# Seven block products for eight in every projection of a pooling and mLSTM layer, with the mLSTM core as a stage of its own

## The chip, the core and the metric

The kernel runs on one core of a Trainium2 chip. The metric is device time in microseconds (us); lower is better. Every time here is that of one launch, and the profile shows one execution. The five engines are TensorE (PE; its weight loads are PEld), VectorE (DVE), ScalarE (ACT), GpSimd (POOL) and SyncE (SP), which issues all DMAs of both kernels.

## The reference, cut

One layer on x, 4096 rows by 1024 channels. A norm, one input projection of five column blocks, two branches, one output projection, a residual and a final norm.

```
proj = rmsnorm(x, norm_w) @ w_in                  # 1024 -> 5 * 1024
pool_x, pool_z, m_x, m_z, m_o = split(proj)       # 1024 columns each
y_pool  = pool_mixer(pool_x, ...) * silu(pool_z)  # trailing means of 2/4/8/16 rows, a map per group
xc = silu(causal_conv(m_x, 4 taps));  q, k, v = small block maps of xc, xc, m_x
h  = mlstm_chunkwise(q, k, v, gates)              # 4 heads of 256, chunks of 128 rows, state handed on
y_mlstm = (headnorm(sigmoid(m_o) * h) + m_skip * xc) * silu(m_z)
out = rmsnorm(x + concat(y_pool, y_mlstm) @ w_out, final_norm_w)
```

So there are seven products of a 4096 by 1024 matrix with a 1024 by 1024 one: five into the branches, two (the halves of w_out) out of them.

## The kernel before, in words

Each float32 operand of a large product is split into a high part (a rounded copy, made by ScalarE) and a low part (the rest, a subtraction on VectorE): `split`, L88 to L90. `mm3` (L114 to L120) then issues three matmuls per pair of 128 by 128 stationary and 128 by 512 moving tiles: high by high, high by low, low by high. L118, L119 and L120 are these three. One of the seven products takes 8 row blocks of 512, 8 column tiles of 128, 8 k tiles and 3 parts, 1536 matmuls 512 wide.

Three stages follow one another, with DRAM between them.

* **Pooling mixer** (L140 to L304). Per block b of 512 rows and column tile j: 24 matmuls for pool_x, into which the group's map is folded beforehand (`fold`, L215), and 24 for pool_z. ScalarE evicts; VectorE makes the window sums (L280), subtracts (L288), multiplies by the gate (L292); POOL carries 16 columns of halo from block to block (L269, L270). `norm_u` (L157) normalises the next block in the background and stores it as `u_d`.
* **mLSTM** (L306 to L689). Per half block of 256 rows `project` makes m_x with matmuls 256 wide (192 of them), and `tail` and `silu` make x_c: three taps by SCALAR_TENSOR_TENSOR on VectorE (L370), SiLU by three functions on ScalarE (L394 to L396) and a product (L397). Per chunk of 128 rows `front` (L462) makes maps (L472, L482), scores (L493), gates, scans (L524, L526) and the decay factors (L552, L561), and `back` (L580) the numerator (L599, L603), the state (L628, L629) and its split copy (L355, L356). `ORDER` (L32) interleaves the steps of a chunk's front (f), the back of the chunk before (b), the next projection (p) and its convolution (c). The tile `qg` exists once: L484 fills it, L493 and L570 read it.
* **Gates, head norm, output** (L691 to L819). m_z and m_o in blocks of 512 rows, sigmoid as tanh, the head norm (L749 to L760), transposes (L726), then the output projection: per 128 rows and 512 columns 48 matmuls, VectorE adds the residual straight from PSUM (L804).

The order of the text sets the priority, not the order on an engine: the framework schedules the instructions when the program is built, and puts an instruction ahead of earlier ones that it expects to be still waiting. Each engine, SP with its DMA issues too, then takes its own list strictly in that order.

## Time and profile before

| | |
|---|---|
| three runs | 3156.46, 3160.59, 3160.87 us; median 3160.59 |
| profiled execution | span 3157.9 us; the page gives no time of its own for it beside the span, which lies 2.7 us under the median |
| pooling mixer | 0 to about 755 us |
| mLSTM | about 755 to 1732 us, 32 chunks |
| gates, head norm | about 1732 to 2443 us |
| output projection | about 2443 to 3158 us |
| mean granted TensorE clock | 0.986 |

How to read it: "busy" is the time in which an engine had an instruction running. Matmuls overlap one another, so the sum of their durations is more than the time they take, and the pace is read from how many start in a stretch. `x` before a number is a count. A row of the windows view gives, for one stretch of time, the length, then for PE, PEld, DVE, ACT and POOL the busy time and the count, then the granted clock, the share of time in which the DMA engines were busy, and GB/s.

### The profile page before, as it was taken

The numbers are of one execution on the slowest core, as the hardware profiler recorded it, in microseconds if no ns is written. First come the engines' busy times: TensorE is split into PE (matmuls) and PEld (weight loads), VectorE is DVE, ScalarE is ACT, GpSimd is POOL, SyncE is SP. The second block draws the span as 40 slices with busy tenths as digits, with TensorE's granted clock in tenths as the row PEclk, the third lists the DMA queues.
The fourth block names the chain that finished last, engine by engine and source line by source line (L and its number), as shares of the span: only waits on it lengthen the run. The fifth ranks groups of instructions, "written<-read, shape, count | busy, mean of one in ns | idle before, by whom it ended". The sixth has DMA issues, their size and how long they took to land.

```text
span 3157.9 us, 44492 instructions
## 1 busy us (share of the span) xinstructions
PE 3056.9 (97%) x16872; PEld 2659.8 (84%) x16872; DVE 1642.0 (52%) x3726; ACT 1162.2 (37%) x2464; POOL 573.8 (18%) x811
## 2 busy tenths in 40 slices
PE   7999999999899999999999999999999999999999
PEld 6888888888898998998998888888888788888887
DVE  5554444544788788888887443334436422222221
ACT  4221122223677677767776222222113311111111
POOL 1010010101354445444543000000000000000000
PEclk9999999999999999999999999999999999999999
DMA  6221111222111111112133223333215523222231
GB/s 210 87 77 70 61 67 60 77 97 75 61 55 58 51 54 62 50 51 64 51 91 112 76 93 107 107 107 107 68 59 173 184 100 107 94 92 96 94 107 50
DMA packets 189607, 273.57 MB, mean 87 GB/s; under 512 B 17232, under 2 KB 111952, under 8 KB 189392
## 3 DMA queue, kind: packets, MB, share of 16 engines
q1 hardware_dynamic: 189392, 270.72, 25.5%
q8 instruction: 133, 2.18, 0.3%
q14 instruction: 82, 0.67, 0.1%
HBM read 168.96 MB, written 101.71 MB: 86 GB/s over the span
## 4 chain that ended last, share of the span: by engine, by line
PE 86%; DVE 6%; DMA 3%; ACT 3%; issue 1%; SPq 1%; POOL 0%; POOLq 0%; DVEq 0%; ACTq 0%
PE acc L118 24%; PE acc L119 24%; PE acc L120 24%; DVE xc L370 3%; PE mm L603 2%; PE mm L628 2%; PE map L482 2%; PE mm L599 1%; DMA sk<-xc_d 1%; PE map L472 1%; PE map L493 1%; DMA ws<-in_w_out_dram 1%; PE acc L236 1%; DVE c L629 1%; PE tp L726 0%
## 5 line engine op out<-in xcount | busy, mean ns | idle before, releaser
L118 PE MATMUL acc<-u,w 128*128 128x512 f32 (+1 forms) x2592 | 907.3, 351 | 3.8 <-ACT mx L617 1.7
L120 PE MATMUL acc<-u,w 128*128 128x512 f32 (+1 forms) x2592 | 897.5, 346 | 0.0
L119 PE MATMUL acc<-u,w 128*128 128x512 f32 (+1 forms) x2592 | 895.5, 346 | 0.0
L118 PE MATMUL acc<-w,u 128*128 128x512 f32 x1536 | 598.4, 390 | 3.8 <-ACT w L89 2.8
L119 PE MATMUL acc<-w,u 128*128 128x512 f32 x1536 | 598.1, 390 | 0.2 <-DVE w L90 0.2
L120 PE MATMUL acc<-w,u 128*128 128x512 f32 x1536 | 597.5, 390 | 0.0
L118 PEld LDWEIGHTS acc<-u,w 128*128 128x128 f32 x2592 | 495.2, 191 | 64.2 <-ACT u L89 4.1
L119 PEld LDWEIGHTS acc<-u,w 128*128 128x128 f32 x2592 | 495.7, 191 | 58.6 <-DVE u L90 1.1
L120 PEld LDWEIGHTS acc<-u,w 128*128 128x128 f32 x2592 | 495.5, 191 | 57.4
L118 PEld LDWEIGHTS acc<-w,u 128*128 128x128 f32 x1536 | 288.5, 188 | 65.5 <-ACT w L89 3.6
L120 PEld LDWEIGHTS acc<-w,u 128*128 128x128 f32 x1536 | 288.9, 188 | 60.4 <-DVE u L790 0.6
L119 PEld LDWEIGHTS acc<-w,u 128*128 128x128 f32 x1536 | 288.6, 188 | 60.6 <-DVE w L90 0.7
L370 DVE SCALAR_TENSOR_TENSOR xc<-mx,col,xc 128x256 f32<-128x256 f32 x384 | 220.6, 632 | 30.5 <-POOL mx L447 22.3
L804 DVE TENSOR_TENSOR st<-acc,st 128x512 f32<-128x512 f32 x64 | 44.3, 692 | 364.9 <-PE acc L120 364.9
L356 POOL TENSOR_TENSOR cs<-c,cs 128x516 fp32r<-128x516 f32 x124 | 176.4, 1423 | 232.0 <-ACT cs L355 208.2
L757 POOL TENSOR_TENSOR rs<-rs,nhalf 128x2 f32<-128x2 f32 x64 | 44.6, 697 | 660.6 <-DVE rs L756 660.6
L789 ACT CAST u<-u 128x512 fp32r<-128x512 f32 x128 | 77.6, 619 | 230.7 <-PE acc L119 187.2
L811 ACT ACTIVATE sk<-st 128x1024 bf16<-128x1024 f32 x31 | 32.8, 1058 | 311.4 <-DVE st L804 311.4
L815 POOL TENSOR_TENSOR rso<-ssq,nhalf 128x1 f32<-128x1 f32 x32 | 17.4, 543 | 701.9 <-DVE ssq L812 701.9
L749 DVE SCALAR_TENSOR_TENSOR st<-th,st 128x512 f32<-128x512 f32 x64 | 44.3, 692 | 184.8 <-ACT th L747 184.7
L747 ACT ACTIVATE th<-acc 128x512 f32<-128x512 f32 x64 | 38.3, 598 | 273.4 <-PE acc L120 272.9
L599 PE MATMUL mm<-va,st 128*128 128x258 f32 x384 | 82.1, 310 | 52.3 <-DVE st L90 39.8
(181 smaller groups left out, 4201.9 us busy)
## 6 DMA issues: line engine op xcount, KB each, us to landing
u<-u_d SPq DMA_DIRECT2D x128, 256.0 KB, 3.9
st<-in_x_t_dram SPq DMA_DIRECT2D x32, 512.0 KB, 3.5
u_d<-st SPq DMA_DIRECT2D x32, 512.0 KB, 4.2
yp_d<-sg SPq DMA_DIRECT2D x64, 256.0 KB, 2.0
xc_d<-xc SPq DMA_DIRECT2D x64, 256.0 KB, 2.4
st<-h_d SPq DMA_DIRECT2D x32, 512.0 KB, 5.2
sk<-xc_d SPq DMA_DIRECT2D x64, 256.0 KB, 3.8
ym_d<-sg SPq DMA_DIRECT2D x64, 256.0 KB, 3.1
```

The source lines that it names most:

```text
L118: nc.tensor.matmul(ps, lhsT=a[0], rhs=b[0], start=start and k == 0, stop=False)
L119: nc.tensor.matmul(ps, lhsT=a[0], rhs=b[1], start=False, stop=False)
L120: nc.tensor.matmul(ps, lhsT=a[1], rhs=b[0], start=False, stop=stop and k == n - 1)
L356: nc.gpsimd.tensor_tensor(out=t[:, 1], in0=cst[h], in1=t[:, 0].bitcast(F32), op=ALU.subtract)
L370: nc.vector.scalar_tensor_tensor(out=a[:, t], in0=m[:, t, i:i + TB], scalar=conv_w[:, jj * 4 + i:jj * 4 + i + 1], in1=a[:, t], op0=ALU.mul ...
L482: nc.tensor.matmul(ps[:, i, :], lhsT=bqk[:, q * 4 + i, :], rhs=xc[q * 4 + i][:, l0:l0 + P], start=True, stop=True)
L599: nc.tensor.matmul(nps, lhsT=wt[:, w, h, :], rhs=vh[v], start=i == 0, stop=first and i == 2)
L603: nc.tensor.matmul(nps, lhsT=qi[h][:, w, t, :], rhs=cs[:, v, t], start=False, stop=t == 1 and i == 2)
L628: nc.tensor.matmul(upd, lhsT=xw[h][:, w, t * P:(t + 1) * P], rhs=vh[v], start=i == 0, stop=i == 2)
L749: nc.vector.scalar_tensor_tensor(out=hv, in0=th, scalar=1.0, in1=hv, op0=ALU.add, op1=ALU.mult)
L757: nc.gpsimd.tensor_tensor(out=rs, in0=rs, in1=nhalf[:, 0:2], op=ALU.pow)
L789: nc.scalar.copy(out=hi, in_=raw)
```

## The change

All seven products become block products of one Strassen-Winograd level: the left matrix is cut into row and k halves (1024 rows are one round r, so there are four rounds), the right one into k and column halves; seven products of sums of blocks replace eight products of blocks. A `Pass` is one product of 1024 columns (or of a mixture of columns) with seven resident, split weight blocks; `drive` streams the seven sums of the left operand past them. In one pass there are 4 rounds of 14 steps (7 block products, 2 k halves each), a step has 4 tiles q, 2 k tiles and 3 parts: 24 matmuls 512 wide.

Seven passes in this order: gate (pool_z); mix 0 and mix 1, each with half the columns of pool_x and half of m_x, whose items do the pooling, the convolution and SiLU; out 1 (upper half of w_out, added to x, stored as `r_d`); then the mLSTM core alone, which reads m_x and x_c from DRAM (`mx_d`, `xc_d`) and writes `h_d`; then head (m_o, sigmoid, head norm), z (m_z, transposes, skip, product) and out 2 (lower half of w_out, added to `r_d`, final norm). The sums of weights (`stage`) and of left operands (`put_left`) are formed on POOL (in the first norms on VectorE), stored in DRAM and loaded again. `ORDER` loses its p and c steps, and its f and b are arranged anew; `front` and `back` are otherwise as before, with three small changes: their inputs are slices of a loaded block, `mm` has 4 PSUM buffers for 3, `ht` has 2 for 1.

The core of the diff:

```
+A_OF = ("a11", "s2", "a12", "s3", "s1", "a22", "s4")
+B_OF = ("b11", "t2", "b21", "t3", "t1", "t4", "b22")
+AHEAD = 3
...
+            for k in range(0, 4, 2):
+                raw = lo[:, k:k + 2].bitcast(F32)
+                nc.sync.dma_start(out=raw, in_=self.wt_d[i][:, k:k + 2, :])
+                split(raw, hi[:, k:k + 2], lo[:, k:k + 2])
...
+    def drive(passes, ring, w2p, psp, background, after=None):
...
+        def fetch(t):
+            n, r, i, kh = steps[t]
+            hi = ring.tile([P, 2, T], F32R, name="sr")
+            lo = ring.tile([P, 2, T], F32R, name="sr")
+            raw = lo.bitcast(F32)
+            nc.sync.dma_start(out=raw, in_=passes[n].left[r][i][:, 2 * kh:2 * kh + 2, :])
+            split(raw, hi, lo)
...
+            for v in range(t, min(t + AHEAD, len(steps))):
+                if v not in got:
+                    fetch(v)
...
+            chain = "abab" "cbc"[i]
...
+            for q in range(4):
...
+                mm3(ps, pairs, start=kh == 0 and i in (0, 1, 4), stop=kh == 1, skip=True)
+                if kh == 1:
+                    f = p.items[q].after(r, i, ps)
...
+            if i == 0:
+                self.s1 = self.tile()
+                nc.scalar.copy(out=v(self.s1), in_=ps)
+            elif i == 1:
+                self.u2 = self.tile()
+                nc.vector.tensor_tensor(out=v(self.u2), in0=ps, in1=v(self.s1), op=ALU.add)
+            elif i == 2:
+                return self.done(r, 0, 0, self.first(ps))
...
+                elif (rh, ch) == (0, 1):
+                    self.mix(r, 0, 1, t)
+                    self.mix(r, 1, 1, self.u3)
+                    v = self.view
+                    put_left(yp_d[r], self.c, v(self.c11), v(t), v(self.s1), v(self.u3), xp, nc.gpsimd)
...
+                for i in range(3):
+                    nc.vector.scalar_tensor_tensor(out=a, in0=m[:, HALO - 3 + i:HALO - 3 + i + T],
...
+        norm_first()
+        for _ in p_gate.stage(xp, nc.gpsimd):
+            pass
+        for g in range(H):
+            fold(g)
+        for i in range(NP):
+            p_gate.load(i, w2p)
...
+            if n == 0 and r + 1 < NR:
+                for _ in range({0: 1, 1: 1, 2: 1, 3: 1, 6: 1, 7: 1, 8: 1, 9: 1, 10: 2}.get(m, 0)):
+                    next(norms[r])
+            if n < 3 and m in ((11, 12) if n == 0 else (4, 11)):
+                next(staged)
+
+        drive([p_gate, *p_mix, p_out1], ring, w2p, psp, background, p_o)
...
+        drive([p_o, p_z, p_out2], ring, w2p, psp, lambda n, r, m: None)
```

`stage` takes, per k tile of a half, 4 loads, 4 sums and 7 stores of 128 by 512 tiles, and has four such k steps per pass; `put_left` takes 4 sums and 7 stores. A fetch is one DMA and one split of 128 by 1024 elements; the ring holds four of them, and three are asked for ahead. The seven products of a round accumulate in three groups of four PSUM banks, "a", "b" and "c": products 0 and 2 in a, 1, 3 and 5 in b, 4 and 6 in c. An item evicts after each product: product 0 and 2 by ScalarE, the others by an addition on VectorE. A quadrant of the result is done after products 2, 4, 5 and 6. A pooling item mixes its first quadrant after product 2, the second after product 5 and the last two after product 6; with a window of 2 a quadrant takes 2 VectorE operations (in the first round more), with 4, 8 and 16 it takes 4, 5 and 6. A convolution item handles its quadrants in the same places: halo on POOL, one ScalarE operation, three SCALAR_TENSOR_TENSOR 512 wide, SiLU, and four DMAs. In the last round of a pass the next pass's seven weight blocks are loaded and split.

`norm_next(r)` loads the 16 tiles of a round's x twice, once for the sums of squares (squares on ScalarE, sums on POOL) and once to scale them (VectorE) and form the seven sums (VectorE). A gate item stores silu(pool_z) in `sz_d`, where the pooling items read it.

More of the change, by code (lines that the diff above doesn't have):

```diff
@@ L116, in mm3, with split @@
+    wf_d = [dram.tile([P, D], F32, name=f"wf_d{k}") for k in range(NJ)]
+    def split(raw, hi, lo, eng=None):
+        nc.scalar.copy(out=hi, in_=raw)
+        (eng or nc.vector).tensor_tensor(out=lo, in0=raw, in1=hi.bitcast(F32), op=ALU.subtract)
+    def mm3(ps, pairs, start=True, stop=True, skip=False):
         n = len(pairs)
         for k, (a, b) in enumerate(pairs):
-            nc.tensor.matmul(ps, lhsT=a[0], rhs=b[0], start=start and k == 0, stop=False)
-            nc.tensor.matmul(ps, lhsT=a[0], rhs=b[1], start=False, stop=False)
@@ new lines, in put_left, with new, put @@
+    def put_left(dst, k, a11, a12, a21, a22, pool, eng, shape=None):
+        def new():
+            return pool.tile([P, T], F32, name="x")
+        def put(what, t):
+            nc.sync.dma_start(out=dst[A_OF.index(what)][:, k, :], in_=t)
+        put("a11", a11)
+        put("a12", a12)
+        put("a22", a22)
+        s1 = new()
+        eng.tensor_tensor(out=s1, in0=a21, in1=a22, op=ALU.add)
+        s2 = new()
+        eng.tensor_tensor(out=s2, in0=s1, in1=a11, op=ALU.subtract)
+        put("s2", s2)
+        eng.tensor_tensor(out=a21, in0=a11, in1=a21, op=ALU.subtract)
+        put("s3", a21)
+        put("s1", s1)
+        s4 = new()
+        eng.tensor_tensor(out=s4, in0=a12, in1=s2, op=ALU.subtract)
+        put("s4", s4)
@@ new lines, in tile_hybrid, with stages, background @@
+        p_out2 = Pass("o2", ym_d, halves(out_rows(D), 0), [], True)
+        def stages():
+            for p in (*p_mix, p_out1, p_o, p_z, p_out2):
+                yield from p.stage(xp, nc.gpsimd)
+        norm_first()
+        for _ in p_gate.stage(xp, nc.gpsimd):
+            pass
+        for g in range(H):
+            fold(g)
+        for i in range(NP):
+            p_gate.load(i, w2p)
+        norms = [norm_next(r) for r in range(1, NR)]
+        staged = stages()
+        def background(n, r, m):
+            if n == 0 and r + 1 < NR:
[3 more added lines that the diff above has]
+                next(staged)
@@ new lines, in block @@
+        def block(b):
+            m = inp.tile([P, NJ, TB], F32, name="mx")
+            nc.sync.dma_start(out=m, in_=mx_d[b])
+            c = inp.tile([P, NJ, TB], F32, name="xc")
+            nc.sync.dma_start(out=c, in_=xc_d[b])
+            return m, c
+        bk = None
+        blocks = {0: block(0)}
+        with tc.issue_after(table.ins):
+            for n in range(NC + 1):
+                if n % 2 == 0 and n + 2 < NC:
+                    blocks[n // 2 + 1] = block(n // 2 + 1)
+                fr = Steps(front(n, n % 2, *blocks[n // 2]), 13) if n < NC else None
+                turn = {"f": fr, "b": bk}
+                for what in ORDER[n % 2]:
+                    if turn[what] is not None:
+                        turn[what].step()
+                if bk is not None:
+                    bk.finish()
+                if fr is None:
+                    break
+                bk = Steps(back(n, *fr.finish()), 5 if n + 1 == NC else 13)
+                bk.step()
@@ L822 @@
+        p_o.items = [Head(q) for q in range(4)]
+        p_z.items = [Mixed(c) for c in range(4)]
+        p_out2.items = [Final(q, r_d, out) for q in range(4)]
+        for i in range(4, NP):
+            p_o.load(i, w2p)
+        drive([p_o, p_z, p_out2], ring, w2p, psp, lambda n, r, m: None)
 def kernel(**inputs):
```

853 lines of the change are left out of this document (432 added, 421 removed).

## The prediction

> **What bounds the kernel now.** I read the page first, its engine line, slices and chain.
>
> ```profile
> span 3157.9 us, 44492 instructions
> PE 3056.9 (97%) x16872; PEld 2659.8 (84%) x16872; DVE 1642.0 (52%) x3726; ACT 1162.2 (37%) x2464; POOL 573.8 (18%) x811
> PE   7999999999899999999999999999999999999999
> DVE  5554444544788788888887443334436422222221
> PE 86%; DVE 6%; DMA 3%; ACT 3%; issue 1%; SPq 1%; POOL 0%; POOLq 0%; DVEq 0%; ACTq 0%
> ```
>
> TensorE is busy throughout and makes 86% of the chain that ended last; VectorE comes near it only in the middle, the mLSTM. So fewer matmuls are worth their time wherever the other engines keep up. The windows view, 100 us of the pooling mixer and 588 us of the mLSTM:
>
> ```profile
> 300.00:400.00 100.00, 100.00 (x443) 82.70 (x442) 48.84 (x75) 23.65 (x40) 9.10 (x19) 1.00 0.20 72
> 932.00:1520.00 588.00, 549.79 (x4417) 535.05 (x4416) 476.97 (x1322) 413.58 (x1004) 287.00 (x363) 0.97 0.17 55
> ```
>
> 443 matmuls 512 wide in 100 us is a pace of 0.2257 us. In the mLSTM PE (94%) and VectorE (81%) are both well filled; projections are what fills PE's gaps there.
>
> **The saving.** After the change a step is 24 x 0.2257 = 5.42 us of PE, a round 75.8, a pass 303.4, seven passes 2124 us. Eight products would be 2427: 303 us are saved, if nothing else becomes the bound. What does, stage by stage:
>
> **Start and gate pass.** Rows: two short windows, three stretches of SP's queue, the first scaled tile, two lines of the DMA list, the folds.
>
> ```profile
> 4.00:8.00 4.00, 0.00 (x0) 0.00 (x0) 1.53 (x4) 2.38 (x4) 0.00 (x0) 1.00 1.01 345
> 28.00:32.00 4.00, 4.00 (x20) 3.54 (x19) 3.46 (x6) 1.21 (x2) 0.00 (x0) 1.00 1.04 387
> 1.25 1.96 SPq L163 DMA_DIRECT2D st<-in_x_t_dram  x4
> 5.81 12.96 SPq L101 DMA_DIRECT2D ws<-in_w_in_dram  x4
> 26.56 4.31 SPq L202 DMA_DIRECT2D u_d<-st  x4
> 24.53 0.75 DVE L200 SCALAR_TENSOR_TENSOR st<-st,col,tp 128x512 f32<-128x512 f32 x1 [0.71 <-PE tp L196]
> u<-u_d SPq DMA_DIRECT2D x128, 256.0 KB, 3.9
> u_d<-st SPq DMA_DIRECT2D x32, 512.0 KB, 4.2
> L236 PE MATMUL acc<-w,w 128*128 128x256 f32 x128 | 31.3, 403 | 14.5 <-POOL w L222 14.5
> ```
>
> With all 16 engines busy (share 1.0) the DMAs moved 345 and 387 GB/s; I take 372 (387 over 1.04). Count in units of 256 KB. Start: x 16, sums of x 28, weight sums 44, folds 38, weight blocks 28, in all 154. Gate pass: 56 fetches 112, gates 64, three norms of 60, eight stage steps 88, next weights 28, in all 472. Of the 626, 44 (sums for mix 1) may be late. 582 units are 152.6 MB, 410 us. PE alone would need 303 after a start of some 50: the first scaled tile came at 24.5 us, another half of rows (about 10), three sums, a store (4.2), a load (3.9) and a split follow. The folds' 31 us of PE stay and fall into that start, where PE would stand anyway; if it did not, they would add 31. So the DMAs bound this part: 420, between 353 and 442 (at 345 GB/s). SP issues at 0.49 us each (1.96 for 4): 112 in a round are 55 us, not the bound. The weight loads (L101) went out before the stores of u (L202), which the text has first: the order is by expected readiness, so a store that waits for its sum need not hold up a fetch behind it. What it can hold up on SP, where the order guesses wrong, is the fetch two steps ahead, and behind that the split and PE; this price is in the third rival.
>
> The Trainium skill (DMA: Bandwidth & Descriptors, Specifications) puts the memory's limit per core at about 358 GB/s. By that, 426 us. The row at 387 lies above it, so I stay with the row.
>
> **Mix passes.** The groups of instructions by form, then durations beside POOL:
>
> ```profile
> L817 DVE SCALAR_TENSOR_TENSOR st<-st,rso,fw 128x1024 f32<-128x1024 f32 x31 | 39.8, 1285 | 22.3 <-POOL rso L815 22.3
> L804 DVE TENSOR_TENSOR st<-acc,st 128x512 f32<-128x512 f32 x64 | 44.3, 692 | 364.9 <-PE acc L120 364.9
> L280 DVE TENSOR_TENSOR sum<-sum 128x525 f32<-128x525 f32 x48 | 33.7, 702 | 1.2
> L200 DVE SCALAR_TENSOR_TENSOR st<-st,col,tp 128x512 f32<-128x512 f32 x64 | 43.5, 741 | 16.1 <-PE tp L196 16.1
> L434 POOL TENSOR_TENSOR u<-u 128x512 fp32r<-128x512 f32 x64 | 85.3, 1335 | 105.3 <-ACT u L433 105.3
> ```
>
> ```profile
> 1286.81 2.45 DVE L370 SCALAR_TENSOR_TENSOR xc<-mx,col,xc 128x256 f32<-128x256 f32 x6
> 1332.49 3.11 DVE L370 SCALAR_TENSOR_TENSOR xc<-mx,col,xc 128x256 f32<-128x256 f32 x5
> 1333.43 1.49 POOL L356 TENSOR_TENSOR cs<-c,cs 128x516 fp32r<-128x516 f32 x1 [1.65 <-ACT cs L355]
> L629 DVE SCALAR_TENSOR_TENSOR c<-c,decay,mm x248: 453/470/485, 822.0 to 1724.3; 128x258 f32<-128x258 f32 x124
> ```
>
> VectorE per round: 14 fetch splits of 1024 elements at 1.25 (a little under L817), 17.5; 20 additions from PSUM at 0.69, 13.8; pooling 34 operations (two quadrants each of 2, 4, 5 and 6) at 0.69, 23.5; convolution 24 at 0.70 (L200's 43.5 over 64 is 0.68, its mean 0.74), 16.8. Together 71.6 us beside PE's 75.8. That would fit but for POOL: five taps took 3.11 us with a POOL addition of 1.49 beside them, where six alone took 2.45 (0.41 each): 1.0 us lost, 0.67 per us of POOL. L629, with an input in PSUM, never exceeded 485 ns, so only splits, sums and taps suffer. POOL makes 16 sums per round (two `put_left`, two stage steps) at 1.33, 21.3 us: 14.3 us lost. VectorE then needs 86 us per round, the last round 17.5 more for the weights: 361 us per pass. I take 365, between 303 (PE's pace) and 430 (below): VectorE bounds, 730 for both. DMAs: 88 units per round, 62 us at 372, under it.
>
> **The other passes.** Out 1: VectorE 17.5 and 36 additions, 24.8, far below 75.8; 303 and 5 for the start. Head: fetch 17.5, additions 13.8, and per quadrant
>
> ```profile
> L753 DVE BATCH_NORM_STATS2 stats<-st 128x6 f32<-128x256 f32 x128 | 48.2, 418 | 2.1
> L754 DVE BATCH_NORM_AGGREGATE mv<-stats 128x2 f32<-128x6 f32 x128 | 19.2, 173 | 0.0
> L726 PE MATMUL tp<-ident,st 128*128 128x128 f32 x256 | 36.2, 274 | 4.3 <-DVE sk L727 4.2
> ```
>
> a product (0.69), two of each of these (1.2) and two small ones (0.3), 2.2 x 16 = 35: 66 us, it fits; 303 and 9 for bursts. Z: the 256 transposes stay (about 30 us, by L726's 36.2 with overlap), 303 and 30 and 5. Out 2: 308. The tail stays, 10.
>
> **The core alone.** The chain of waits in order of time (ten pairs of chunks apart), the groups that leave, two stretches of one chunk, and 24 projection matmuls in a row (first, and what follows the last):
>
> ```profile
> 932.42 1.85 PE map L472 x16
> 1518.76 1.85 PE map L472 x16
> 1306.66 0.28 PE L118 MATMUL acc<-u,w 128*128 128x256 f32 x1
> 1309.53 0.88 PE L628 MATMUL mm<-va,ws 128*128 128x258 f32 x6
> L370 DVE SCALAR_TENSOR_TENSOR xc<-mx,col,xc 128x256 f32<-128x256 f32 x384 | 220.6, 632 | 30.5 <-POOL mx L447 22.3 <-ACT xc L453 7.8 <-POOL mhal L449 0.2
> L397 DVE TENSOR_TENSOR xc<-xc,sgm 128x512 f32<-128x512 f32 x68 | 48.3, 710 | 5.3 <-ACT sgm L396 5.2
> 1287.48 0.63 ACT L484 COPY qg<-map 128x512 f32<-128x512 f32 x1
> 1306.26 1.08 DVE L570 TENSOR_TENSOR qr<-qg,inter 128x256 f32<-128x256 f32 x3
> ```
>
> A chunk takes 586.3/20 = 29.3 us. Per chunk PE is busy 27.4 (549.79/588 x 29.3) and loses 96 matmuls at 0.12 (2.87/24), 11.5: 15.9 stay. VectorE is busy 23.8 and loses 6.9 (220.6/32) and 1.4: 15.5. So no chunk under 15.9. From above: `qg` is one tile, and from its first write to its last read went 19.9 us (1287.48 to 1307.34); with the next q'' matmuls in front (0.9) it is 20.8, if none of the waits behind projections goes. Two engines at 15.5 to 15.9 in strict order will not run full, and some waits do go: 19.5, nearer the chain. 32 x 19.5 = 624, 20 to fill and drain, 25 and 10 to change stages (tables, maps, first weights; bounded by 0 and by the 50 of the start): 679.
>
> **The sum.** 420 + 730 + 308 + 679 + 312 + 338 + 308 + 10 = 3105 us of span, against 3157.9; the median stood 2.7 above the span, so 3108.
>
> One rule speaks against part of it. Two windows:
>
> ```profile
> 2476.00:2480.00 4.00, 1.40 (x7) 0.72 (x5) 1.40 (x3) 1.24 (x2) 0.00 (x0) 1.00 0.67 242
> 2480.00:2484.00 4.00, 4.00 (x12) 3.13 (x11) 1.86 (x3) 1.24 (x2) 0.00 (x0) 0.57 0.65 228
> ```
>
> After 2.6 us without PE the granted clock was 0.57 for 4 us: 12 matmuls for 18, 1.4 us more. The mix passes' 62 us of waiting each, in two gaps per round, would cost 16 x 1.4 = 22 us; where VectorE is the bound this hides behind it, so I count none and keep 22 for the range. The Trainium skill (TensorE: Matmul & The Clock Gate, The HAM clock gate) says the clock halves after an idle window of about 3.4 us; by that, 1.7 per gap, 27 us.
>
> **The rivals.**
> * **All at PE's pace** (faster): the DMAs overlap better than the rows show and POOL's sums fall beside ScalarE-bound moments. 353 + 607 + 308 + 599 (17 per chunk) + 312 + 338 + 308 + 10 = 2835. For it: 71.6 is below 75.8 without POOL. Against: the L370 rows. 0.17.
> * **The core bound by its chain** (slower): without projections nothing fills PE's gaps, and each hand-over between engines in strict order shows. At 24 us per chunk, between 20.8 and today's 29.3, 144 us are added: 3249. It decides from 21.2 us per chunk (52.9 us over 32). For it: the 19.9 measured. Against: part of it was waiting behind the projections. 0.20. The Trainium skill (Perfetto Trace Analysis, Identifying the Most-Contended Engine) advises to interleave regimes with different bounds; this change takes such an interleaving apart.
> * **Bursts in the mix passes** (slower): after product 6 VectorE has 4 additions, 22 pooling operations and 12 taps, 26 us, while fetches reach two steps, 10.8 us, ahead. PE would stand 15 us there and some 6 after products 2 and 5. A round then is between 97 (75.8 and 21) and 107 (86 and 21); with 103, and 17.5 for the weights, a pass is 430, and both add 130: 3235. It decides from 392 per pass (26 more, twice). For it: the stores of a burst and the fetches behind them share SP's one queue. Against: in the trace L101 passed L202, so splits and fetches can be put ahead of taps. 0.15.
>
> **Chances.** Forecast (3000 to 3150) 0.43, the first rival 0.17: faster 0.60. The two slower rivals 0.35. The same, within 0.2% (6 us, what a measurement here can tell), 0.05. The range goes to half of the first rival and takes in both slower ones: 2890 to 3300. The likeliest case's own is 3000 to 3150.
>
> **What would show it.** Gate pass with DMA share near 1 and PE under 85%; mix passes 350 to 380 us with VectorE over 90% and taps of 512 over 0.9 us; out 1 and out 2 at 443 matmuls per 100 us; the core's L472 groups 19 to 20 us apart. Wrong if passes other than gate and mix stand below PE's pace, if a chunk exceeds 21.2, or if PE waits for VectorE over 90 us per mix pass.

## The result and the profile after

The changed kernel takes 3595.9 us (median of four runs, 3589.0 to 3596.9) against 3159.6 (four runs, 3156.5 to 3160.9): a ratio of 1.138, 95% interval 1.136 to 1.139. It is 436 us slower; 3108 was forecast, and the range ended at 3300. The profiled execution took 3595.1 us, its span 3593.4.

The page of the changed kernel: span, engine line, slices of PE.

```profile
span 3593.4 us, 42393 instructions
PE 2897.7 (81%) x13800; PEld 2404.4 (67%) x13800; DVE 2322.8 (65%) x4217; ACT 1428.7 (40%) x2513; POOL 1014.0 (28%) x1029
PE   3467468977779777699978888876999899986998
```

PE has 13800 matmuls instead of 16872, the eighth product's among those that left. But its share of the span fell from 97% to 81%, and the holes lie mostly in the first 17 slices. To see them by stage I cut the trace where the projection matmuls change pass: a pass is 1344 of them, and the 1st, 1345th and so on mark the limits. The windows view, in order: start, gate, mix 1 and mix 2 (the first and the second mix pass, mix 0 and mix 1 of the kernel), out 1, core with its stage changes, head, z, out 2 with the tail. Its columns are the stretch, its length, busy time of PE, PEld, DVE, ACT and POOL, the granted clock, the share of the DMA engines and GB/s.

```profile
0.00:149.70 149.70, 37.13 (x137) 29.03 (x137) 53.98 (x75) 36.81 (x52) 28.46 (x29) 0.73 0.80 274
149.70:627.40 477.70, 340.66 (x1368) 268.98 (x1369) 228.67 (x278) 154.72 (x212) 116.05 (x81) 0.85 0.77 252
627.40:1033.30 405.90, 331.23 (x1346) 264.68 (x1344) 293.66 (x355) 128.27 (x160) 172.41 (x171) 0.91 0.72 232
1033.30:1462.80 429.50, 344.18 (x1345) 272.31 (x1345) 318.19 (x392) 133.37 (x167) 199.72 (x192) 0.88 0.72 233
1462.80:1809.50 346.70, 312.38 (x1344) 255.53 (x1344) 203.01 (x251) 78.43 (x78) 21.02 (x20) 0.95 0.66 220
1809.50:2506.50 697.00, 547.05 (x3978) 512.48 (x3976) 545.71 (x1664) 449.22 (x1167) 311.09 (x376) 0.91 0.24 85
2506.50:2839.60 333.10, 318.76 (x1344) 259.08 (x1344) 223.04 (x557) 173.45 (x259) 52.80 (x58) 0.96 0.61 193
2839.60:3234.20 394.60, 352.22 (x1583) 285.53 (x1584) 236.74 (x308) 170.07 (x230) 71.41 (x55) 0.94 0.77 246
3234.20:3593.40 359.20, 314.07 (x1363) 256.75 (x1361) 219.83 (x343) 104.35 (x191) 41.03 (x48) 0.94 0.58 195
```

| Term of the sum | forecast | measured | difference |
|---|---|---|---|
| start and gate pass | 420 | 627.4 | +207 |
| two mix passes | 730 | 835.4 | +105 |
| out 1 | 308 | 346.7 | +39 |
| core and stage changes | 679 | 697.0 | +18 |
| head | 312 | 333.1 | +21 |
| z | 338 | 394.6 | +57 |
| out 2 and tail | 318 | 359.2 | +41 |

No engine is full in the stages that cost most. In the gate pass PE has 71% of the time, VectorE 48%, the DMA engines 77%; in the mix passes VectorE has 72 and 74%. Such a stage is held up by the order of its work, and the queue that shows it best is SP's, which issues every transfer. PE's waits in the gate pass are nearly all of one kind, for a fetch that came late to its cast (engine, line, releaser, us, times, longest):

```profile
PE ps L111 <- ACT sr L104: 146.8, 11, 22.7
```

First, SP about a change of round in the gate pass (start, length, entry; a row holds entries in a row of one kind, with their waits):

```profile
254.47 1.44 SPq L131 DMA_DIRECT2D x<-wf_d  x2
...
284.52 2.40 SPq L355 DMA_DIRECT2D x<-in_x_t_dram  x4
...
377.10 0.38 SPq L196 DMA_DIRECT2D sr<-us_d  x1
380.13 7.96 SPq L169 DMA_DIRECT2D us_d<-x  x7
...
395.71 0.43 SPq L196 DMA_DIRECT2D sr<-us_d  x1
...
418.70 0.52 SPq L196 DMA_DIRECT2D sr<-us_d  x1
```

The norm before has put its last store just ahead of the row at 254.5; two steps of weight sums follow, and only at 284.5 does the norm of the next round begin with its first load of x. It ends at 388.1 with its last store: 103.6 us, where PE needs 75.8 for a round. Behind it come two more steps of weight sums (L131, L136). The first fetches of the next round stand among all these entries: the first ahead of the norm's last stores, the second behind them and behind the loads of a step of sums, the third behind the rest of both steps. They go out 18.6 and 23.0 us apart, where a step of PE lasts 5.4. Second, SP and ScalarE in mix 1, where PE stood still:

```profile
758.24 9.07 SPq L136 DMA_DIRECT2D wt_o<-x  x7
767.41 0.40 SPq L196 DMA_DIRECT2D sr<-us_d  x1
```

```profile
773.39 1.04 ACT L104 CAST sr<-sr 128x1024 fp32r<-128x1024 f32 x1 [4.42 <-DMA sr<-us_d]
```

The seven stores of a step of weight sums stand on SP for 9 us: three need only their loads, four need additions on GpSimd, and one of these waits 4.4 us. The fetch behind them goes out at 767.4, is there at 773.4, and only then comes the cast, the split and the matmul. The views of waits of the two mix passes, SP's first, with some lines left out, then PE's:

```profile
SPq L518 <- ACT wk L516: 94.5, 46, 6.1
SPq L136 <- POOL x L145: 69.3, 15, 5.6
...
SPq L169 <- POOL x L175: 42.4, 8, 8.6
...
SPq L169 <- POOL x L177: 33.7, 14, 8.0
```

```profile
PE ps L111 <- ACT sr L104: 84.9, 21, 10.0
PE ps L112 <- DVE sr L105: 74.8, 24, 11.3
```

The first line of PE's is a fetch that came late to its cast, the second a split that VectorE reached late: 160 us in both passes, about evenly. SP's longest line is not one of GpSimd's: stores of x_c wait for ScalarE's SiLU (L516). Of the edits below only e1 takes the fetches from behind these as well. Out 1 has its loss in its first round, when the last round of mix 2 is still being worked off; from the second round on it ran at the old pace, as the forecast had it:

```profile
1600.00:1700.00 100.00, 100.00 (x443) 82.78 (x442) 53.29 (x68) 18.94 (x18) 0.00 (x0) 1.00 0.61 200
```

### The profile page after: what moved, and what is told of

Read it like the earlier page. It is cut to its first block, busy times and chain, and to the rows that moved or that the text cites. A ratio compares the mean times of both kernels' runs of the same rounds, so it can differ in the third digit from the quotient of the medians.

```text
span 3593.4 us, 42393 instructions
## 1 busy us (share of the span) xinstructions
PE 2897.7 (81%) x13800; PEld 2404.4 (67%) x13800; DVE 2322.8 (65%) x4217; ACT 1428.7 (40%) x2513; POOL 1014.0 (28%) x1029
## 4 chain that ended last, share of the span: by engine, by line
PE 29%; DVE 14%; DMA 5%; ACT 4%; POOL 3%; issue 3%; SPq 1%; POOLq 0%; DVEq 0%; ACTq 0%
PE ps L111 8%; PE ps L113 8%; PE ps L112 8%; DMA sr<-us_d 2%; DVE c L819 2%; DVE ws L779 1%; PE mm L796 1%; DVE ch L988 1%; POOL rs L918 1%; PE map L665 1%; DVE dm L757 1%; DVE st L105 1%; DMA x<-hn_d 1%; DVE ch L273 1%; ACT dm L754 1%
## 5 line engine op out<-in xcount | busy, mean ns | idle before, releaser
L111 PE MATMUL ps<-sr,w 128*128 128x512 f32 x1792 | 726.3, 414 | 250.7 <-ACT sr L104 250.5
L105 DVE TENSOR_TENSOR sr<-sr 128x1024 fp32r<-128x1024 f32 x392 | 501.2, 1280 | 562.2 <-ACT sr L104 561.3
L104 ACT CAST sr<-sr 128x1024 fp32r<-128x1024 f32 x392 | 411.2, 1049 | 1033.7 <-DMA sr<-us_d 621.5
L112 PE MATMUL ps<-sr,w 128*128 128x512 f32 x1792 | 736.7, 411 | 77.9 <-DVE sr L105 77.2
L113 PE MATMUL ps<-sr,w 128*128 128x512 f32 x1792 | 727.6, 406 | 0.0
L111 PEld LDWEIGHTS ps<-sr,w 128*128 128x128 f32 x1792 | 354.6, 200 | 341.2 <-ACT sr L104 266.5
L111 PE MATMUL ps<-w,sr 128*128 128x512 f32 x1344 | 533.3, 397 | 58.2 <-ACT sr L104 58.2
L113 PE MATMUL ps<-w,sr 128*128 128x512 f32 x1344 | 530.3, 395 | 9.4 <-DVE sr L105 9.4
L112 PE MATMUL ps<-w,sr 128*128 128x512 f32 x1344 | 531.1, 395 | 0.0
L112 PEld LDWEIGHTS ps<-sr,w 128*128 128x128 f32 x1792 | 357.1, 199 | 178.1 <-DVE sr L105 102.5
L113 PEld LDWEIGHTS ps<-sr,w 128*128 128x128 f32 x1792 | 356.0, 199 | 74.9
L111 PEld LDWEIGHTS ps<-w,sr 128*128 128x128 f32 x1344 | 257.7, 192 | 116.7 <-ACT sr L104 63.5
L113 PEld LDWEIGHTS ps<-w,sr 128*128 128x128 f32 x1344 | 256.7, 191 | 69.7 <-DVE sr L105 16.0
L112 PEld LDWEIGHTS ps<-w,sr 128*128 128x128 f32 x1344 | 257.3, 191 | 53.3
L273 DVE TENSOR_TENSOR ch<-ps,ch 128x512 f32<-128x512 f32 x336 | 224.0, 682 | 66.0 <-PE ps L113 65.8
L105 DVE TENSOR_TENSOR w<-w,w 128x1024 fp32r<-128x1024 f32 x98 | 122.0, 1250 | 150.2 <-ACT w L104 149.4
L513 DVE SCALAR_TENSOR_TENSOR wk<-ch,col,wk 128x512 f32<-128x512 f32 x192 | 180.5, 971 | 1.8 <-ACT wk L510 0.9
L447 POOL COPY halo<-ch 128x16 f32<-128x16 f32 x128 | 120.5, 949 | 202.9 <-DVE ch L273 157.1
```

The costliest lines, as they stand in the source:

```text
L104: nc.scalar.copy(out=hi, in_=raw)
L105: (eng or nc.vector).tensor_tensor(out=lo, in0=raw, in1=hi.bitcast(F32), op=ALU.subtract)
L111: nc.tensor.matmul(ps, lhsT=a[0], rhs=b[0], start=start and k == 0, stop=False, skip_group_check=skip)
L112: nc.tensor.matmul(ps, lhsT=a[0], rhs=b[1], start=False, stop=False, skip_group_check=skip)
L113: nc.tensor.matmul(ps, lhsT=a[1], rhs=b[0], start=False, stop=stop and k == n - 1, skip_group_check=skip)
L273: nc.vector.tensor_tensor(out=v(t), in0=ps, in1=v(t), op=ALU.add)
```

## The experiments

Every theory below names what a stage waits for. **Bytes**: the DMA engines are the bound, as the forecast had it for the gate pass. **VectorE**: its work, lengthened by GpSimd's, is the bound, as forecast for the mix passes. **Queue**: fetches stand on SP behind stores that wait. **Bursts and reach** (the third rival): work piled up on VectorE, with fetches only two steps ahead. Times are medians, with the ratio to the kernel before where there was more than one execution; stages are cut as above.

| Run | us | ratio, 95% interval | start | gate | mix 1 | mix 2 | out 1 |
|---|---|---|---|---|---|---|---|
| the change | 3595.9 | 1.136 to 1.139 | 150 | 478 | 406 | 430 | 347 |
| e1 fetches on ScalarE's queue | 3558.9 | 1.125 to 1.129 | 136 | 473 | 393 | 413 | 345 |
| e2 stores on GpSimd's queue | 3502.5 | 1.107 to 1.110 | 96 | 483 | 387 | 404 | 347 |
| e3 no weight sums | 3386.0 | 1.070 to 1.074 | 149 | 398 | 347 | 369 | 346 |
| e4 norm early | 3585.5 | 1.133 to 1.137 | 147 | 466 | 411 | 429 | 348 |
| e6 more x tiles | 3622.4 | 1.145 to 1.151 | 151 | 482 | 415 | 436 | 356 |
| e7 sums on VectorE | 3463.3 | 1.095 to 1.099 | 150 | 463 | 354 | 370 | 338 |
| e8 three steps ahead | 3535.0 | 1.118 to 1.121 | 149 | 462 | 388 | 413 | 349 |
| e9 start reordered | 3587.1 | 1.134 to 1.138 | 148 | 474 | 408 | 429 | 347 |
| g1 16.8 MB more | 3604.1 | 1.139 to 1.143 | 150 | 481 | 413 | 431 | 348 |
| b1 e2, e7 and e8 | 3435.0 | 1.086 to 1.090 | 96 | 464 | 362 | 375 | 352 |
| b2 and weight sums spread | 3421.5 | 1.081 to 1.085 | 95 | 445 | 343 | 378 | 371 |
| b3 and start reordered | 3423.8 | 1.081 to 1.085 | 134 | 420 | 337 | 375 | 368 |
| h1 b2 and norm early | 3422.6 | 1.082 to 1.085 | 98 | 449 | 339 | 375 | 372 |
| h2 no later norms | 3428.5 | one execution | 148 | 320 | 393 | 433 | 348 |
| h3 e7 without taps | 3444.4 | one execution | 150 | 465 | 343 | 362 | 338 |
| h4 more tiles for z | 3609.4 | one execution | 149 | 476 | 407 | 429 | 346 |
| h5 b2, norms without pause | 3411.6 | 1.077 to 1.082 | 96 | 446 | 344 | 378 | 361 |
| h6 norm's sums on VectorE | 3585.0 | 1.133 to 1.137 | 150 | 475 | 401 | 428 | 346 |

**e1, the fetches on another queue.**

```diff
-            nc.sync.dma_start(out=raw, in_=passes[n].left[r][i]...
+            nc.scalar.dma_start(out=raw, in_=passes[n].left[r][i]...
```

> Only the fetches of the streamed operand (L196) go from SP's queue to ScalarE's; bytes, sums and stores stay. Queue theory (a fetch stands on SP behind stores that wait for sums on POOL or VectorE): the stalls of about 25 us in each round of the mix passes shrink by half or more, those of some 30 us in the first rounds of out 1 and out 2 go, the gate pass changes little since its first fetches wait for the stores themselves; 3596 becomes 3380 to 3480. Bytes theory (the DMA engines at 0.7 to 0.87 busy are the bound): within 30 us of 3596. VectorE theory (its work beside POOL's is the bound in the mix passes): within 30 us of 3596.

37 us were gained, a third of what the queue theory had said at least. The waits of PE in the mix passes tell where the rest went:

```profile
PE ps L112 <- DVE sr L105: 88.9, 30, 7.8
PE ps L111 <- DVE ch L265: 43.3, 6, 11.1
PE ps L111 <- ACT sr L104: 11.2, 7, 3.9
```

The wait for late fetches fell from 84.9 to 11.2, and VectorE's took its place: 132 us of splits and of additions that clear a bank. Two waits stood one behind the other.

**e2, the stores on GpSimd's queue.**

```diff
-            nc.sync.dma_start(out=dst[A_OF.index(what)][:, k, :], in_=t)
+            nc.gpsimd.dma_start(out=dst[A_OF.index(what)][:, k, :], in_=t)
```

and the same in `stage`.

> The stores of the weight sums and of the left operands' sums (L136, L169) go from SP's queue to GpSimd's, the engine that makes most of the sums; bytes and sums stay. Queue theory: nothing that waits for a sum stands ahead of a fetch any more, the mix passes fall from 405 and 430 us to 330 to 370 each, the gate pass from 478 to 400 or less; 3596 becomes 3300 to 3450. Bytes theory: within 30 us of 3596. VectorE theory: no gain, or slower by up to 60 us since GpSimd has more to do beside VectorE.

93 us were gained, and the places were not those expected: 53 in the start, where the gate pass's blocks now go out beside the norm's stores, 45 in the mix passes, none in the gate pass. In the mix passes PE's two waits changed as in e1: those for late fetches fell from 84.9 to 22.6 us, those for splits rose from 74.8 to 89.7.

**e3, no weight sums for the later passes.** The six passes use the gate pass's blocks.

```diff
-        staged = stages()
+        for p in (*p_mix, p_out1, p_o, p_z, p_out2):
+            p.wt_d = p_gate.wt_d
...
-            if n < 3 and m in ((11, 12) if n == 0 else (4, 11)):
-                next(staged)
```

> Leaves out the sums of the weights of the last six passes, with their loads and stores (24 steps of 11 transfers of 256 KB, 69 MB of 722, and 96 additions on GpSimd); those passes use the gate pass's blocks. Queue theory: half of the stalls of the mix passes goes (those behind L136), those behind L169 stay; 3596 becomes 3430 to 3520. Bytes theory: 69 MB at 330 GB/s are 209 us, most of it in the gate and mix passes: 3380 to 3430. VectorE theory: 64 additions of 1.4 us leave the mix passes, at 0.67 of VectorE per us of GpSimd 60 us: 3520 to 3550.

It took 210 us off, the very figure of the bytes theory (209), and alone it would have settled the case for it. That the figure was a coincidence shows in two runs below: g1 moves more bytes in the gate pass at hardly any cost, and in the mix passes, where e3 gained 120, e7 gained 111 with the same bytes.

**e4, the norm earlier.**

```diff
-{0: 1, 1: 1, 2: 1, 3: 1, 6: 1, 7: 1, 8: 1, 9: 1, 10: 2}
+{0: 2, 1: 2, 2: 2, 3: 1, 4: 1, 5: 1, 6: 1}
```

> The same ten background steps of the next round's normalisation in the gate pass, ended by step 6 of a round instead of step 10; nothing else changes. The three round changes of the gate pass lost 48, 55 and 52 us (155) against PE's pace. Lateness theory (the round's first fetch waits for stores that were begun too late): 100 to 155 of them go, 3596 becomes 3440 to 3500. Bytes theory: the same transfers take the same time wherever they stand in the round: within 30 us of 3596.

The lateness theory falls: the stalls moved within the round and kept all but 12 us of their sum.

**e6, more x tiles.**

```diff
-            tc.tile_pool(name="a_ring", bufs=8) as ring, \
+            tc.tile_pool(name="a_ring", bufs=6) as ring, \
-            tc.tile_pool(name="a_x", bufs=8) as xp, \
+            tc.tile_pool(name="a_x", bufs=12) as xp, \
```

> Twelve x tiles instead of eight, paid for with six ring tiles instead of eight (three fetches in flight instead of four). Slot theory (the norms and the weight sums of the gate pass run one after the other through eight tiles, each waiting for its loads and stores to land, 105 to 130 us per round where PE needs 76): the gate pass falls from 478 to 400 to 430, 3596 becomes 3520 to 3550. Bytes theory (the DMA engines are the bound there): the gate pass stays within 15 us of 478 and the total within 30 of 3596, or slower by the smaller ring.

Slower by 27 us, the gate pass as long as before. The four x tiles were paid for with two of the ring's, so the run shows only that this exchange does not pay; more tiles by themselves were not tested.

**e7, the sums on VectorE.**

```diff
-                yield from p.stage(xp, nc.gpsimd)
+                yield from p.stage(xp, nc.vector)
...
-                    put_left(yp_d[r], ..., v(self.u3), xp, nc.gpsimd)
+                    put_left(yp_d[r], ..., v(self.u3), xp, nc.vector)
```

> All sums of weights and left operands that GpSimd makes go to VectorE; loads, stores and queues stay. Contention theory (an addition of 1.4 us on GpSimd takes 0.9 us from VectorE, while VectorE itself makes it in 0.69; and the stores behind it on SP leave earlier): the mix passes fall from 835 to 720 to 790, 3596 becomes 3470 to 3560. Work theory (VectorE is the bound and gets 16 x 0.69 = 11 us per round more): the mix passes rise by 50 to 90, 3640 to 3690. Queue theory: only the time that stores wait for sums halves, 30 to 60 us gained.

133 us were gained, a little more than the contention theory had, 111 of them in the mix passes. The taps by their line, of the changed kernel and then of e7 (shortest, median and longest, ns):

```profile
L513 DVE SCALAR_TENSOR_TENSOR wk<-ch,col,wk x192: 731/742/1860, 672.1 to 1507.5; 128x512 f32<-128x512 f32 x192
```

```profile
L513 DVE SCALAR_TENSOR_TENSOR wk<-ch,col,wk x192: 729/743/754, 656.3 to 1377.9; 128x512 f32<-128x512 f32 x192
```

The median is the same; the long ones, up to 1860, which made the mean 971, are gone with GpSimd's additions. VectorE's busy time in the two passes:

```profile
612.70:966.80 354.10, 324.21 (x1345) 260.59 (x1344) 288.90 (x409) 129.23 (x162) 105.59 (x110) 0.95 0.84 266
966.80:1337.20 370.40, 328.79 (x1346) 262.98 (x1345) 318.74 (x456) 133.08 (x166) 134.49 (x128) 0.93 0.83 270
```

It does 118 operations more (865 against 747) and is busy for 607.6 us instead of 611.8. Operations of VectorE overlap a little where they follow one another: in h6 four of 0.69 us begin at 304.38, 304.98, 305.58 and 306.18. At 0.60 each the new ones are 71 us, so the old ones cost 75 less, while GpSimd's time fell by 132: 0.57 us per us, an estimate. So the sums cost VectorE nothing. But its total did not fall, and the gain is in waits: SP stood for 145.4 us in the three GpSimd lines shown above, which are gone; for the same sums made by VectorE (L145, L175, L177) it stood 29.2. PE's two waits went from 84.9 and 74.8 to

```profile
PE ps L111 <- ACT sr L104: 43.1, 14, 9.7
PE ps L112 <- DVE sr L105: 24.1, 16, 3.5
```

**e8, three steps ahead.**

```diff
-AHEAD = 3
+AHEAD = 4
```

> Fetches three steps ahead instead of two; the four pairs of ring tiles suffice. In the trace PE's stalls fall on flights of fetches (issued, not yet landed) for about 30 us in each mix pass and 50 in the gate pass, on VectorE reaching the split late for 21 and 33. Reach theory (two steps, 10.8 us, are too short for a fetch behind a burst of stores, a cast and a split): 3596 becomes 3480 to 3540. VectorE theory (splits stand behind the taps whatever their fetch does): the waits for flights become waits for the split, 3570 to 3600.

61 us were gained, as the reach theory had it: 35 in the mix passes, 15 in the gate pass, 19 in out 2.

**e9, the start in another order.** In `norm_first` the loads of x come first, and behind them the gate pass's weight sums, for which `stage` is told to take its tiles from the ring:

```diff
+            for _ in p_gate.stage(xp, nc.gpsimd, lambda: ring.tile([P, 2, T], F32R, name="sr").bitcast(F32)):
+                pass
...
         norm_first()
-        for _ in p_gate.stage(xp, nc.gpsimd):
-            pass
+        for i in range(4):
+            p_gate.load(i, w2p)
         for g in range(H):
             fold(g)
-        for i in range(NP):
+        for i in range(4, NP):
             p_gate.load(i, w2p)
```

> The start in another order: the gate pass's weight sums are made right behind the first loads of x, in the ring's tiles instead of the x tiles, and the folds come behind the first four weight loads. Bytes and sums stay. Order theory (the start's 150 us are norm, weight sums, folds and loads one after the other, at 0.77 of the DMA engines): the first matmul of the gate pass comes at 85 to 110 instead of 150, and the gain stays: 3535 to 3560. Bytes theory: what is moved from the start falls into the gate pass, which is the longer for it: 3580 to 3600.

The first matmul of the pass came at 148.1, so the edit did not do what it was for: SP now held the norm's stores behind the weight sums' stores, and the first fetch behind the folds'. Between the theories it tells nothing.

**g1, more bytes.**

```diff
+            if n == 0 and m in (3, 5, 7, 9):
+                nc.sync.dma_start(out=more_d[4 * r + (m - 3) // 2], in_=p_gate.slots[6][0].bitcast(F32))
```

> Adds four stores of 1 MB to each round of the gate pass (a resident weight block written to DRAM where nobody reads it): 16.8 MB in 16 transfers, nothing else. Bytes theory (the gate pass runs at what the DMA engines give, about 250 GB/s there): 16.8 MB add 55 to 67 us to its 478. Serial theory (the pass is bound by the chain of loads, sums, stores and fetches in SP's order, and the DMA engines have a quarter of their time to spare): under 25 us.

The gate pass, by the windows view:

```profile
150.10:631.20 481.10, 356.39 (x1368) 276.79 (x1369) 225.74 (x279) 154.20 (x212) 109.46 (x76) 0.85 0.84 284
```

It moves 284 GB/s instead of 252 and takes 3.4 us longer. The pass is not bound by bytes.

**b1, b2, b3, the single edits together.** b1 is e2, e7 and e8; b2 also gives the gate pass five steps of weight sums instead of eight, mix 1 four and out 1 seven; b3 adds e9's start. The edit of b2:

```diff
-            if n < 3 and m in ((11, 12) if n == 0 else (4, 11)):
-                next(staged)
+            if m in (((11, 12), (12,), (12,), (12,))[r] if n == 0 else (11,) if n == 1 else (4, 11)):
+                next(staged, None)
```

> The three single edits together: stores of sums on GpSimd's queue, all later sums on VectorE, fetches three steps ahead. Alone they gained 93, 132 and 61 us. If they remove different waits (queue, contention, reach), 3596 less 286: 3300 to 3330. If they remove the same stalls of the mix passes in different ways, little more than the best two: 3350 to 3420.

> As the run of the three edits together, and the 24 steps of weight sums spread over the passes otherwise: five in the gate pass instead of eight, four, eight and seven in mix 1, mix 2 and out 1. Serial and bytes theories alike: the gate pass gives back some 13 us per step moved (39), out 1 has room for seven: 25 to 45 us below that run. If the gate pass is bound by its norms alone: within 10 us of it.

> As the run before, and the start in the other order (weight sums behind the first loads of x, in ring tiles; folds behind the first four weight loads). With the stores on GpSimd's queue SP no longer stands behind them: first matmul of the gate pass at 65 to 80 instead of 96. If the gate pass is then the longer for the folds, the total moves by less than 10 us, else 15 to 30 below the run before.

b1 gained 161 where the parts give 287: they remove the same stalls in different ways. b2 gained 13.5 more: 19 each in the gate pass and mix 1, of which out 1 took 19 back. In b3 the start is 39 us longer and the gate pass 26 shorter: the same work elsewhere.

**h1, h2, what holds the gate pass up.** h1 is b2 with e4's table; h2 is the changed kernel without the norms of rounds 2 to 4:

```diff
+        us_d[1:] = us_d[:1] * (NR - 1)
...
-            if n == 0 and r + 1 < NR:
-                for _ in range({0: 1, 1: 1, 2: 1, 3: 1, 6: 1, 7: 1, 8: 1, 9: 1, 10: 2}.get(m, 0)):
-                    next(norms[r])
```

> As the run with the spread weight sums, and the norm of the next round ended by step 6 of a round instead of step 10 (the edit that gained only 12 us in the gate pass when it stood alone). Theory of two things in line (the norm and the weight sums each hold up the fetches of the next round on SP; with one of them out of the way the other one counts): the gate pass falls from 445 to 370 to 410, the total to 3345 to 3385. If lateness is not it: within 15 us of 3422.

> The changed kernel without the norms of rounds 2 to 4 (left out: their loads, sums and stores, 45 MB; every round reads the first round's operand). Theory of two things in line: the weight sums alone, eight steps of some 13 us, can be fetched past in part; the gate pass falls from 478 to 330 to 380. Norm theory (only the norms hold the pass up): 303 to 325. Weight-sum theory (only they do): 400 and more.

h1 moved nothing, again. h2's gate pass:

```profile
147.80:467.60 319.80, 313.04 (x1344) 255.34 (x1345) 134.96 (x147) 114.87 (x146) 55.51 (x42) 0.98 0.79 253
```

Without the norms PE fills it to 98%, though all eight steps of weight sums are still in it. Without the weight sums (e3) it was 398: its first three rounds took 104 to 107 us, its norms 102 to 112. With both, the norm (103.6) and the two steps of sums ahead of it (254.5 to 284.5, 30) give 134, and the round took 131 (255.2 to 386.4). They are in line: the sums come free only where no norm is in the way. By its bands h2 alone, at 320, spoke for the norms as the only cause; e3, which keeps the norms and took 80 us off the pass, speaks against it.

**h5, h6, the norm itself.** h5 is b2 with the norms without pause between them and their sums of squares on VectorE; h6 is the changed kernel with those sums on VectorE alone:

```diff
-                        nc.gpsimd.tensor_tensor(out=ss[:, h], in0=ss[:, h], in1=t, op=ALU.add)
+                        nc.vector.tensor_tensor(out=ss[:, h], in0=ss[:, h], in1=t, op=ALU.add)
```

h5 has this edit too, and

```diff
-        norms = [norm_next(r) for r in range(1, NR)]
+        norms = (s for r in range(1, NR) for s in norm_next(r))
...
+            if n == 0:
+                for _ in range((("22111111011110", "11111101111000", "11111100000000", "0" * 14)[r][m] > "0") + (r == 0 and m < 2)):
+                    next(norms, None)
```

> As the run with the spread weight sums, the norms of rounds 2 to 4 run one behind the other without a pause (the first half of a norm already in the round before), and their sums of squares go from GpSimd to VectorE. Chain theory (one norm takes some 104 us from its first load to its last store, and PE's round is 76): three norms are 312 less about 10 each, 282 us, which four rounds can hide better; the gate pass falls from 445 to 380 to 415, the total to 3360 to 3390. If it is SP's order that holds the fetches up whatever the norm does: within 15 us of 3422.

> The changed kernel with one edit: the 14 sums of squares of a norm on VectorE (0.69) instead of GpSimd (1.3 to 2.2, 20 us in line from 292.6 to 315.4 in the second round). Chain theory (norm and weight sums follow each other, and every us taken from the norm is taken from the round): 8 to 12 us per round less, 3596 becomes 3560 to 3572. If the chain has slack: within 10 us of 3596.

Both fell short: 10 and 11 us, the gate pass within 3 us of where it was. In h5 the three norms took 308 us from the first load to the last store instead of 331 in b2, and the pass was no shorter for it. That is what was expected if SP's order holds the fetches up, and SP's waits in h5's second round (from 205 to 365 us) show where:

```profile
SPq L355 <- DMA us_d<-x: 39.5, 14, 10.1
```

Loads of x wait there until a store of the norm has landed, which frees a tile. The norm for the third round put its last store at 338.6; the first fetch of that round went out at 352.1, behind sixteen loads of the norm after it.

In h6 the sums of squares had time to spare. The last sums of the second round's norm, the split of the first half's sum and the first matmuls on it, in the changed kernel and in h6:

```profile
301.71 13.71 POOL L389 TENSOR_TENSOR ss<-ss,x 128x512 f32<-128x512 f32 x8
307.50 1.78 DVE L105 TENSOR_TENSOR x<-ss,x 128x512 fp32r<-128x512 f32 x1
320.80 0.62 PE L330 MATMUL ps<-x,ones_r 128*128 128x512 f32 x2
```

```profile
309.12 2.29 DVE L389 TENSOR_TENSOR ss<-ss,x 128x512 f32<-128x512 f32 x3
308.51 0.69 DVE L105 TENSOR_TENSOR x<-ss,x 128x512 fp32r<-128x512 f32 x1
321.64 0.62 PE L330 MATMUL ps<-x,ones_r 128*128 128x512 f32 x2
```

The first half's sum is split at 309.3 and at 309.2, and in both PE comes to it some 12 us later, after a step of the round. The second half's sums end at 311.4 instead of 315.4, and its cast on ScalarE starts at 328.4 instead of 327.8. So a norm is not a chain of its own: PE's steps pace it too.

**h3, h4, what is left in mix and z.** h3 is e7 without the convolution's taps; h4 is the changed kernel with other pools:

```diff
-                for i in range(3):
-                    nc.vector.scalar_tensor_tensor(out=a, in0=m[:, HALO - 3 + i:HALO - 3 + i + T],
...
-            tc.tile_pool(name="c_ch", bufs=22) as chp, \
-            tc.tile_pool(name="c_x", bufs=6) as xp, \
+            tc.tile_pool(name="c_ch", bufs=18) as chp, \
+            tc.tile_pool(name="c_x", bufs=10) as xp, \
```

> As the run with all sums on VectorE (mix passes 354 and 370), without the convolution's three taps (left out: 24 operations of 742 ns per round, 17.8 us of VectorE; nothing else). Burst theory (after the seventh product VectorE has 26 us of work standing ahead of the next splits): the mix passes fall by 75 to 110 together, to near PE's 607, and the first round of out 1 by 10 or more. If the mix passes are held up by transfers by now: less than 25.

> The changed kernel with ten instead of six x tiles behind the core (and 18 instead of 22 chunk tiles). Slot theory for z (PE stands 48 us in line behind transposes whose input was loaded late, since two of six tiles per quadrant are taken): z falls from 395 to 350 to 370. If the loads are late since SP has them behind other entries: within 8 us of 395.

h3 gained 19 us in its one execution, the mix passes 20: by then VectorE's burst does not set the time. PE's waits in its mix passes are for fetches, with 4.5 us left for splits:

```profile
PE ps L111 <- ACT sr L104: 55.1, 14, 14.0
```

In h4 z took 395.8, as before, so the number of tiles isn't its cause.

## Why the prediction was wrong

**What bounds the kernel, the saving.** Right as far as PE goes: where nothing else holds it up, in out 1, its pace is 443 matmuls in 100 us, and a round of seven products takes 76 us.

**Start and gate pass.** Here the step failed that took the DMAs as the bound and added their bytes to 410 us. No stage ran at 372 GB/s; the gate pass ran at 252 with the engines 77% busy, and 16.8 MB more cost 3.4 us (g1). By the 358 GB/s of the Trainium skill (DMA: Bandwidth & Descriptors, Specifications) the bytes would have taken 426, an estimate; this pass came nowhere near that limit, so nothing here tests it. What the step lacked was the length of the background work as a chain. A norm loads its tiles, waits for PE's matmuls, loads them again, scales, sums and stores. Eighteen traces hold three norms each, and 53 of the 54 took 89 to 116 us from the first load to the last store (b3's first, which begins within the start, took 149); a round of PE is 76. The next round's fetches need its stores, and stand on SP behind its entries and those of the weight sums. No rival made this part longer, and it has the largest difference of all. The start failed the same way; the pass's first matmul came at 149.7. SP:

```profile
57.17 2.29 SPq L131 DMA_DIRECT2D x<-in_w_in_dram  x4
...
69.94 1.90 SPq L131 DMA_DIRECT2D x<-in_w_in_dram  x4
...
138.66 0.32 SPq L196 DMA_DIRECT2D sr<-us_d  x1
```

Some 50 us were put on it, by a chain that left out the four weight-sum steps. They begin behind the norm's stores, at 57.2, and the second follows the first at 12.8 us; most stores of the folds and the weight loads come behind them, and then the first fetch.

"The order is by expected readiness, so a store that waits for its sum need not hold up a fetch behind it" was wrong. The rows at 758.24 and 767.41 are that very case. The row of before that it rested on showed an order that had come out well once; it could not show what SP does with hundreds of stores that wait.

**Mix passes.** The price of GpSimd's work on VectorE was near: 0.67 us per us was forecast, 0.57 comes out of e7. Taps over 0.9 us were forecast too, and came: 971 ns in the mean. The Trainium skill (SBUF — State Buffer, Who interferes with whom) has an operation of VectorE with two inputs in SBUF contend with one of GpSimd that reads SBUF. The two rows of taps in e7 agree with it.

That VectorE is the bound was wrong: it was busy for 294 and 318 us, not 361, in passes of 406 and 430. One reason for the 361 is that it adds full durations, which overlap (e7). PE's waits for VectorE's splits, 74.8 us in both passes, stayed under the 90 per pass named as a sign of error; PE waited longer, 84.9 us, for late fetches, which the sum had at nothing. The third rival's figure, 430 per pass, came closest; its mechanism was part of it. Bursts and the short reach are there (e8 gained 35 in these passes, e1 turned fetch waits into split waits). About half, 111 of the 228 us above PE's 607, went with GpSimd's sums (e7). That edit takes away two things at once, the contention and the stores that wait on SP for slow sums; e2, which takes the stores off SP and leaves the contention, gained 45. What each is worth alone beyond that was not separated.

**Core alone.** The figure was right: 679 was forecast, 697 measured. The first matmuls of a chunk, with the first and last start:

```profile
L665 PE MATMUL map<-bvg,mx x512: 279/279/574, 1832.8 to 2463.7; 128*128 128x136 f32 x171
```

They come in 32 groups of 16; the last group begins 2.3 us before its last start, at 2461.4, which makes 628.6 over 31, 20.3 us per chunk against 19.5, under the 21.2 at which the second rival decides. That it came near the forecast was in part luck, since the chain of `qg`, from which 19.5 was taken, does not set it. A chunk's first write and last read of it, and the next chunk's first write:

```profile
1914.03 1.08 ACT L677 COPY qg<-map 128x512 f32<-128x512 f32 x2
1929.28 1.42 DVE L763 TENSOR_TENSOR qr<-qg,inter 128x256 f32<-128x256 f32 x4
1934.49 1.08 ACT L677 COPY qg<-map 128x512 f32<-128x512 f32 x2
```

The tile is in use for 16.7 us and then free for 3.8. What does set a chunk was not tested. The Trainium skill (Perfetto Trace Analysis, Optimization Strategy, where the advice stands) says that interleaving regimes with different bounds may gain time; here the stage without its interleaving came out 18 us above its forecast, and most of the loss lies elsewhere.

**Head, z, outs.** Out 1's 39 us lie in its first round, while SP still issued the burst of mix 2's last round:

```profile
1477.42 0.48 SPq L196 DMA_DIRECT2D sr<-yp_d  x1
...
1511.35 0.43 SPq L196 DMA_DIRECT2D sr<-yp_d  x1
```

34 us lie between two fetches. The head stood 30 us above PE's 303: 14 idle, most of them at the first steps of its rounds, and 15 in longer matmuls (318.8 us busy). In z the transposes by themselves are near their price (38.5 us busy, 30 forecast), but PE stood at them for their loads, 48.4 us that the forecast had at nothing (busy, mean, idle before and its releasers):

```profile
L955 PE MATMUL ps<-ident,x 128*128 128x128 f32 x256 | 38.5, 288 | 50.0 <-DMA x<-hn_d 48.4 <-DVE w L105 0.9 <-DVE ch L273 0.6
```

Only 20.9 of them lie in z, which lost another 20.1 to late fetches. The rest lies in the first round of out 2 (110.6 us), where z's last transposes stand, and is most of out 2's 41:

```profile
PE ps L955 <- DMA x<-hn_d: 27.5, 3, 12.7
```

The head and out 2 are read from the trace; no run was made for them.

**The clock.** 22 us were kept for the range and none put in the sum. The windows show more: a granted clock of 0.85 in the gate pass, and in the two mix passes 675.4 us busy for 607 of work. With the 160 us of waits these 68 make up the 228 above 607. They look like a consequence of the waits and not a cause of their own, since in e7 both fell, the waits by 93 and the busy time by 22; no run tested the clock by itself.

**What stays open.** That the norms hold the gate pass up is shown (h2), and that the weight sums add to it (e3). What in a norm sets the price is open: bytes (g1), its stores' queue (e2), its start (e4, h1), pauses (h5) and its sums of squares (h6) are each ruled out as the only cause. Its tiles are not: e6 took them from the ring, and h5's loads wait for free ones. More tiles with the stores off SP, which might let a norm's blocks overlap, were not run. Why z's loads come late is open too. No version tried beats the kernel before: the best, h5, is at 1.080.

## What to carry to other kernels

A saving on the engine that fills the span is worth only what the feeding can follow: before adding up bytes and busy times per pass, add up the longest chain of load, wait, sum and store that one round must get through, and lay it beside the round. Read the one queue that issues the transfers as an engine of its own: a store that waits for a sum takes the time of every fetch behind it. A run that hits the figure of a theory does not prove it, as e3 shows; add the suspected cost by itself, as g1 did.

## What was not expected of the hardware

An operation of VectorE beside additions on GpSimd (1481.41 to 1484.70) took 1.76 us where its like took 0.7, so that handing 16 sums per round to the less busy engine cost VectorE as much as making them itself.

```profile
1481.81 1.76 DVE L472 TENSOR_TENSOR wk<-ch 128x527 f32<-128x527 f32 x1
```

And no queue alone was the limit of the gate pass: with fetches on ScalarE's queue (e1) or stores on GpSimd's (e2), it kept its length within 5 us.
